# Layer 1's attention is begun inside the last query projection, its short logits share a bank, and one head's scaling changes engines

## The chip, the cores and the metric

The kernel runs on one core of a Trainium2 chip. The metric is the device time of one execution in microseconds (us). Beside the timed runs there is one execution recorded by the hardware profiler.

## The reference

Two layers of a decoder trunk act on 512 tokens of width 1024, in float32. Layer 0 mixes tokens by stick-breaking attention and a short convolution, and ends with a SwiGLU. Layer 1, where the change lies, projects the normalized input to 16 query heads, 4 key and value heads of 64, and to a small indexer with 8 heads, whose score picks 128 keys for each query:

```
dots  = einsum(q_idx, k_idx) * 64 ** -0.5
score = einsum(w_idx * 8 ** -0.5, relu(dots)), causal
idx   = top_k(score, 128)
q, k  = rms_norm(q) * q_gain, rms_norm(k) * k_gain
logits = einsum(q, k[idx]) * 64 ** -0.5 + rel_bias[bucket(q_pos - idx)]
out   = softmax(logits) @ v[idx]
x     = x + out @ w_out
```

Four query heads share one key and value head. A SwiGLU follows.

## The kernel before

All products are made of halves: each float32 operand is cut into a high part, rounded to the type that TensorE takes at speed, and a low part, the difference, and a product is three matmuls. `proj_fm` and `proj_tm` are the dense projections, and `slot` is called after each group of three such matmuls (with 512 columns). A slot is the unit of the written order: `after(n, fn, key)` puts a piece of work behind the n-th slot from now, the pieces of one slot in order of `key`. In layer 1 the scheduler is off for TensorE, VectorE, ScalarE and GpSimd, so each of them executes in the order in which the program issues; DMAs of the SP queue are placed by the scheduler.

In `layer1_mix` the stages stand in this order. The indexer's projections come first, then its scores (`dot`, `add_score`) and the choice of the largest 128 for the query blocks 1 to 3 (`largest`, `take`, lines 934 to 940), which ends in the matrices `mask`. Meanwhile keys and values, and the first eight query heads, are projected. `squares` and `head_norm` make the query norm: squares on ScalarE (line 966), a sum on VectorE (967), a reciprocal root on ScalarE (979), four small operations on VectorE, a product on GpSimd (987). `turn_q` then transposes the queries (line 999) and `stack` cuts them into halves (lines 494 and 498), the low halves of the first eight heads on GpSimd. The second eight query heads are projected next, in 32 slots (`ev_q1`, line 1173, copies its four results out), and their norm and turns follow.

Attention runs over 16 units: `order` goes through the four groups g of four heads, and in each through the four query blocks qb. A unit n has the heads 4g to 4g+3, each with (qb+1)·128 keys. Its pieces hang on b = 4n + 32 - EARLY slots, counted from the start of the last query projection:

- `logits` (lines 1064 to 1088): two matmuls of one head into a bank "z" (lines 507 and 508), of which there are two; for qb above 0 a third that adds the mask (1084); then a reduce on VectorE (1085) that adds the head's position bias, writes the sum to the tile L and the row maximum to `mx`. The bias tile of a head is loaded by a DMA of the SP queue in the unit with qb = 0 (line 1078). There are four such tiles, so the load of head h+4 waits for the last reduce of head h.
- `exps`: VectorE negates `mx` (1093), ScalarE takes four exponentials with row sums (1095).
- `norms`: one reciprocal of the four sums on VectorE (1102), and the scaling of four heads, on GpSimd (1105) or VectorE (1110) by the table NORM_POOL.
- `turn_p`: four transposes of one key block (1118), a cast on ScalarE (1129), and LAG_LO slots later the low part on VectorE (1130).
- `prod`: six matmuls with the values (lines 105 to 107) into a bank "po"; `keep` copies the unit's output out (1150, 1151).

When the query projection is over, slots pass without projection matmuls until the output projection's first half starts, 50 slots after the first unit's.

Of the kernel before, what the change touches and what calls it, by code (L numbers as in the profile page):

```python
# [8 lines left out]
F32 = mybir.dt.float32  # L9
F32R = mybir.dt.float32r  # L10
ALU = mybir.AluOpType
# [4 lines left out]
P = 128  # L16
S = 512
# [14 lines left out]
LAG_K, T1P, B2, LAG_KLO, P1 = 2, 3, 'adbc', 2, 0  # L32
EARLY, SQ_ACT = 3, 256
DOT_PACE = 1
DBL_ACT, K_POOL = True, True
PACE = (4.8, 5.0, 5.3)
NORM_POOL, NORM_ACT = (1,), (3,)
Q_POOL = ((1,), (2, 3))
EPS = 1e-6
NEG = -1e30  # L40
FILL = -3e38
# [1 line left out]
ARENA_KB = 104.5  # L43
X_SPANS = ((0, 1), (1, 2), (2, 4), (4, 6), (6, 8))

EARLY = 2
T1P = 4
LAG_K = 3
NORM_POOL = (0, 1, 3)
NORM_ACT = ()  # L50
LAG_CH = 4
LAG_TQ = 5
# [24 lines left out]
class Net:  # L77
# [762 lines left out]
    def layer1_mix(self):  # L840
        nc, I, tc = self.nc, self.I, self.tc
# [10 lines left out]
        qs, qsf = self.R(72.5, 16, S)  # L852
# [3 lines left out]
        with ExitStack() as es:  # L856
            sp = es.enter_context(tc.tile_pool(name="l1", bufs=2))
# [3 lines left out]
                    for qb in range(TB)]  # L861
            score = [None] + [wide[qb]()[:, 0] for qb in (1, 2)] + [self.ssq]
            mask = [None] + [sp.tile([P, (qb + 1) * P], F32R, name=f"mask{qb}", bufs=1)
                             for qb in (1, 2, 3)]
            eye = self.eye
# [77 lines left out]
            for qb, pace in zip((1, 2, 3), PACE):  # L943
                for r in range(16):
                    t = dots[qb] - self.slots + int(pace * r)
# [73 lines left out]
            t = head_norm(hk, [t[:, :, 1] for t in d], [t[:, :, 0] for t in d], 4, 1)  # L1019
# [40 lines left out]
            t = head_norm(h0, heads(q0[0]), heads(q0[0]), 8, 1.7)  # L1060
# [3 lines left out]
            order = [(qb, g) for g in range(4) for qb in range(TB)]  # L1064
            bias, us = {}, [{} for _ in order]

            def logits(n, r):
                (qb, g), u = order[n], us[n]
                nk = (qb + 1) * P
                t = slice(qb * P, nk)  # L1070
                h = 4 * g + r
                if r == 0:
                    u["mx"] = sp.tile([P, TB], F32, name="mx", bufs=3)
                    u["sm"] = sp.tile([P, TB], F32, name="sm", bufs=3)
                    u["ls"] = wide[qb]()
                if not qb:
                    bias[h] = sp.tile([P, S], F32, name="bias", tag="rb", bufs=4)
                    nc.sync.dma_start(bias[h], bass.AP(tensor=self.F.tensor,
                                                       offset=self.F.offset + h * 640,
                                                       ap=[[1, P], [1, S]]))  # L1080
                z = self.bank("z", "z")[:, 0:nk]
                self.qk(z, qs[:, h, t], kh[:, g, 0:nk], kl[:, g, 0:nk], not qb)
                if qb:
                    nc.tensor.matmul(z, eye, mask[qb], start=False, stop=True)  # L1084
                nc.vector.tensor_tensor_reduce(out=u["ls"][:, r], in0=z,  # L1085
                                               in1=bias[h][:, 0:nk][:, ::-1],
                                               scale=1.0, scalar=FILL, op0=ALU.add,
                                               op1=ALU.max, accum_out=u["mx"][:, r:r + 1])

            def exps(n, rs):  # L1090
                ls, mx, sm = us[n]["ls"], us[n]["mx"], us[n]["sm"]
                if rs[0] == 0:
                    nc.vector.tensor_scalar(mx, mx, -1.0, None, op0=ALU.mult)
                for r in rs:
                    nc.scalar.activation(ls[:, r], ls[:, r], AF.Exp, bias=mx[:, r:r + 1],
                                         accum_out=sm[:, r:r + 1])

            def norms(n, rs):
# [4 lines left out]
                for r in rs:  # L1103
                    if r in NORM_POOL:
                        nc.gpsimd.tensor_tensor(ls[:, r], ls[:, r],
# [39 lines left out]
            def keep(n):  # L1145
                qb, g = order[n]
                t = slice(qb * P, (qb + 1) * P)
                c = slice(2 * g, 2 * g + 2)
                po = us[n]["po"].rearrange("p (c q) -> p c q", c=2)
                nc.scalar.copy(ah[:, c, t], po)  # L1150
                self.after(LAG_K, lambda: nc.vector.tensor_tensor(
                    al[:, c, t], po, ahf[:, c, t], op=ALU.subtract), -2)

            for n, (qb, g) in enumerate(order):
                b = 4 * n + 32 - EARLY
                for r in range(4):
                    self.after(b + r, lambda n=n, r=r: logits(n, r), 0)
                for r in range(4):
                    self.after(b + 4 + r // EXPS, lambda n=n, r=r: exps(n, (r,)), 0.5)
                    self.after(b + LAG_N + r // 2, lambda n=n, r=r: norms(n, (r,)), 3)  # L1160
                for kb in range(qb + 1):
                    self.after(b + LAG_C + kb, lambda n=n, kb=kb: turn_p(n, kb), 1)
                    self.after(b + LAG_C + LAG_P + kb, lambda n=n, kb=kb: prod(n, kb), 2)
                self.after(b + LAG_C + LAG_P + qb + 1, lambda n=n: keep(n), -1)
            start = self.slots + 32 - EARLY

# [10 lines left out]
            t = head_norm(h1, heads(q1), heads(q1), 8, 1)  # L1177
# [62 lines left out]
```

## Time and profile before

| | us |
|---|---|
| median of 3 runs | 1211.86 (1211.82 to 1212.19) |
| profiled execution, its time | 1214.13 |
| profiled execution, its span | 1212.4 |
| TensorE busy | 1189.0 |
| VectorE busy | 652.9 |
| ScalarE busy | 480.1 |
| GpSimd busy | 143.8 |

The span goes from the first to the last instruction of the profiled execution; times in the trace count from its start. Matmuls are pipelined and the trace models their ends, so the starts are the safer numbers. The attention of layer 1 begins at 698 us. An idle time in brackets stands before the instruction, with what ended it.

### The profile page before, as it was taken

The numbers are of one execution on the slowest core, as the hardware profiler recorded it, in microseconds if no ns is written. First come the engines' busy times: TensorE is split into PE (matmuls) and PEld (weight loads), VectorE is DVE, ScalarE is ACT, GpSimd is POOL, SyncE is SP. The second block draws the span as 40 slices with busy tenths as digits, with TensorE's granted clock in tenths as the row PEclk, the third lists the DMA queues.
The fourth block names the chain that finished last, engine by engine and source line by source line (L and its number), as shares of the span: only waits on it lengthen the run. The fifth ranks groups of instructions, "written<-read, shape, count | busy, mean of one in ns | idle before, by whom it ended". The sixth has DMA issues, their size and how long they took to land.

```text
span 1212.4 us, 14654 instructions
## 1 busy us (share of the span) xinstructions
PE 1189.0 (98%) x5547; PEld 978.5 (81%) x5547; DVE 652.9 (54%) x1067; ACT 480.1 (40%) x797; POOL 143.8 (12%) x217
## 2 busy tenths in 40 slices
PE   9999999999999999999999989999999999999998
PEld 7777878888888888888788868888888888888886
DVE  5679965655545443333379977745444343342222
ACT  5556634543434332222253577534332322322120
POOL 1234300200000000011001554312000000000000
PEclk9999999999999999999999999999999999999999
DMA  5322125878887632232346432223333333332430
GB/s 191 92 70 70 53 84 190 277 248 281 284 273 262 226 92 96 96 96 78 124 150 232 157 104 70 71 78 126 91 89 90 103 87 102 89 104 88 129 97 35
DMA packets 118583, 159.86 MB, mean 132 GB/s; under 512 B 6292, under 2 KB 91840, under 8 KB 118512
## 3 DMA queue, kind: packets, MB, share of 16 engines
q1 hardware_dynamic: 117712, 157.73, 40.1%
q10 hardware_dynamic: 800, 1.18, 0.3%
q8 instruction: 44, 0.72, 0.2%
q14 instruction: 27, 0.22, 0.1%
HBM read 131.00 MB, written 27.89 MB: 131 GB/s over the span
## 4 chain that ended last, share of the span: by engine, by line
PE 89%; DVE 6%; issue 2%; POOL 2%; ACT 0%; DMA 0%; POOLq 0%; DVEq 0%; ACTq 0%
PE acc L105 22%; PE acc L107 21%; PE acc L106 21%; PE acc L234 6%; PE acc L233 6%; PE acc L232 6%; PE pt L1118 1%; PE z L507 1%; PE z L508 1%; DVE om L532 1%; DVE wl L163 1%; PE po L106 1%; PE po L107 1%; DVE be L535 1%; PE po L105 1%
## 5 line engine op out<-in xcount | busy, mean ns | idle before, releaser
L105 PE MATMUL acc<-arena,wh 128*128 128x512 f32 (+2 forms) x1176 | 466.7, 397 | 1.9 <-DVE xT L728 1.0
L107 PE MATMUL acc<-arena,wl 128*128 128x512 f32 (+2 forms) x1176 | 458.2, 390 | 0.1
L106 PE MATMUL acc<-arena,wh 128*128 128x512 f32 (+2 forms) x1176 | 458.0, 389 | 0.0
L163 DVE TENSOR_TENSOR wl<-raw,wh 128x1024 fp32r<-128x1024 f32 (+1 forms) x167 | 202.9, 1215 | 285.3 <-ACT wh L162 285.0
L162 ACT CAST wh<-raw 128x1024 fp32r<-128x1024 f32 (+1 forms) x167 | 173.0, 1036 | 360.5 <-PE acc L106 155.7
L107 PEld LDWEIGHTS acc<-arena,wl 128*128 128x128 f32 (+1 forms) x1176 | 220.4, 187 | 49.9 <-DVE wl L163 0.4
L105 PEld LDWEIGHTS acc<-arena,wh 128*128 128x128 f32 (+1 forms) x1176 | 220.8, 188 | 46.9 <-DVE xT L728 2.1
L106 PEld LDWEIGHTS acc<-arena,wh 128*128 128x128 f32 (+1 forms) x1176 | 220.8, 188 | 43.6 <-issue 0.7
L232 PE MATMUL acc<-wh,arena 128*128 128x512 f32 x272 | 108.8, 400 | 0.0
L234 PE MATMUL acc<-wh,arena 128*128 128x512 f32 x272 | 108.4, 399 | 0.0
L233 PE MATMUL acc<-wl,arena 128*128 128x512 f32 x272 | 108.2, 398 | 0.0
L286 POOL TENSOR_TENSOR ssq<-ssq,sqx 128x512 f32<-128x512 f32 x12 | 18.2, 1520 | 371.7 <-ACT sqx L285 371.7
L234 PEld LDWEIGHTS acc<-wh,arena 128*128 128x128 f32 x272 | 51.5, 189 | 12.2
L815 DVE TENSOR_TENSOR pwl<-praw,pwh 128x1024 fp32r<-128x1024 f32 (+1 forms) x25 | 30.2, 1208 | 57.0 <-ACT pwh L814 57.0
L233 PEld LDWEIGHTS acc<-wl,arena 128*128 128x128 f32 x272 | 51.5, 189 | 11.6
L232 PEld LDWEIGHTS acc<-wh,arena 128*128 128x128 f32 x272 | 51.5, 189 | 11.5
L763 DVE TENSOR_TENSOR ft<-acc,rbc 128x512 f32<-128x512 f32 x44 | 30.0, 690 | 45.7 <-PE acc L107 45.6
L814 ACT CAST pwh<-praw 128x1024 fp32r<-128x1024 f32 (+1 forms) x25 | 25.9, 1036 | 68.5 <-DMA praw<-in_od_w_in_dram 38.2
L765 ACT ACTIVATE fs<-ft 128x512 f32<-128x512 f32 x44 | 27.6, 629 | 51.3 <-DVE ft L763 51.3
L507 PE MATMUL z<-arena 128*128 128x384 f32 (+3 forms) x120 | 40.7, 342 | 6.7 <-DVE mx L1085 4.1
L1085 DVE CUSTOM_DVE_ANT_0 L<-z,bias 128x128 f32<-128x128 f32 (+3 forms) x64 | 30.7, 485 | 22.2 <-PE z L1084 19.6
L770 DVE TENSOR_TENSOR fp<-acc,fs 128x512 f32<-128x512 f32 x44 | 30.4, 690 | 22.7 <-PE acc L107 22.7
(212 smaller groups left out, 1281.0 us busy)
## 6 DMA issues: line engine op xcount, KB each, us to landing
raw<-in_ffn_w_gate_dram SPq DMA_DIRECT2D x44, 512.0 KB, 3.7
raw<-in_ffn_w_up_dram SPq DMA_DIRECT2D x44, 512.0 KB, 3.8
raw<-in_ffn_w_down_dram SPq DMA_DIRECT2D x42, 512.0 KB, 3.7
l1h<-pwh SPq DMA_DIRECT2D x24, 512.0 KB, 2.7
l1l<-pwl SPq DMA_DIRECT2D x24, 512.0 KB, 3.1
wh<-l1h SPq DMA_DIRECT2D x24, 512.0 KB, 4.0
wl<-l1l SPq DMA_DIRECT2D x24, 512.0 KB, 4.5
raw<-in_ev_w_in_dram SPq DMA_DIRECT2D x23, 512.0 KB, 3.9
```

Of the source, the lines that this page charges most:

```text
L105: mm(ps, wh, xh, start=first, stop=False)
L106: mm(ps, wh, xl, start=False, stop=False)
L107: mm(ps, wl, xh, start=False, stop=last)
L162: nc.scalar.copy(wh, raw)
L163: (lo or nc.vector).tensor_tensor(wl, raw, wh.bitcast(F32), op=ALU.subtract)
L232: mm(ps[tb], h[:, t], wh[:, k], start=c == 0, stop=False)
L233: mm(ps[tb], h[:, t], wl[:, k], start=False, stop=False)
L234: mm(ps[tb], l[:, t], wh[:, k], start=False, stop=c == kc - 1)
L507: self.nc.tensor.matmul(z, qs, kd, start=True, stop=False)
L770: nc.vector.tensor_tensor(p, ps, sil[m], op=ALU.mult)
L815: nc.vector.tensor_tensor(l, raw, h.bitcast(F32), op=ALU.subtract)
L1085: nc.vector.tensor_tensor_reduce(out=u["ls"][:, r], in0=z, in1=bias[h][:, 0:nk][:, ::-1], scale=1.0, scalar=FILL, op0=ALU.add, op1=ALU.max ...
```

## The change

EARLY goes from 2 to 11: everything that hangs on b moves 9 slots ahead, against the projections and the query turns, which stay. `logits` takes a tuple of heads: in units with 128 keys all four heads write to one bank and are issued in one slot, in units with 256 keys two and two; the matmuls of all heads of a bank are issued first, then their reduces. `turns`, which picks banks and tiles for the transposes, is set to -1 before the attention. NORM_POOL goes from (0, 1, 3) to (0, 1, 2).

```diff
-EARLY = 2
+EARLY = 11
 T1P = 4
 LAG_K = 3
-NORM_POOL = (0, 1, 3)
+NORM_POOL = (0, 1, 2)
...
-            def logits(n, r):
+            def logits(n, rs):
+
                 (qb, g), u = order[n], us[n]
                 nk = (qb + 1) * P
                 t = slice(qb * P, nk)
-                h = 4 * g + r
-                if r == 0:
+                if rs[0] == 0:
                     u["mx"] = sp.tile([P, TB], F32, name="mx", bufs=3)
                     u["sm"] = sp.tile([P, TB], F32, name="sm", bufs=3)
                     u["ls"] = wide[qb]()
-                if not qb:
-                    bias[h] = sp.tile([P, S], F32, name="bias", tag="rb", bufs=4)
-                    nc.sync.dma_start(bias[h], bass.AP(tensor=self.F.tensor,
-                                                       offset=self.F.offset + h * 640,
-                                                       ap=[[1, P], [1, S]]))
-                z = self.bank("z", "z")[:, 0:nk]
-                self.qk(z, qs[:, h, t], kh[:, g, 0:nk], kl[:, g, 0:nk], not qb)
-                if qb:
-                    nc.tensor.matmul(z, eye, mask[qb], start=False, stop=True)
-                nc.vector.tensor_tensor_reduce(out=u["ls"][:, r], in0=z,
-                                               in1=bias[h][:, 0:nk][:, ::-1],
-                                               scale=1.0, scalar=FILL, op0=ALU.add,
-                                               op1=ALU.max, accum_out=u["mx"][:, r:r + 1])
+                bank = self.bank("z", "z")
+                zs = [bank[:, i * nk:(i + 1) * nk] for i in range(len(rs))]
+                for r, z in zip(rs, zs):
+                    h = 4 * g + r
+                    if not qb:
+                        bias[h] = sp.tile([P, S], F32, name="bias", tag="rb", bufs=4)
+                        nc.sync.dma_start(bias[h], bass.AP(tensor=self.F.tensor,
+                                                           offset=self.F.offset + h * 640,
+                                                           ap=[[1, P], [1, S]]))
+                    self.qk(z, qs[:, h, t], kh[:, g, 0:nk], kl[:, g, 0:nk], not qb)
+                    if qb:
+                        nc.tensor.matmul(z, eye, mask[qb], start=False, stop=True)
+                for r, z in zip(rs, zs):
+                    nc.vector.tensor_tensor_reduce(out=u["ls"][:, r], in0=z,
+                                                   in1=bias[4 * g + r][:, 0:nk][:, ::-1],
+                                                   scale=1.0, scalar=FILL, op0=ALU.add,
+                                                   op1=ALU.max, accum_out=u["mx"][:, r:r + 1])
...
+            self.turns = -1
             for n, (qb, g) in enumerate(order):
                 b = 4 * n + 32 - EARLY
-                for r in range(4):
-                    self.after(b + r, lambda n=n, r=r: logits(n, r), 0)
+                w = (4, 2, 1, 1)[qb]
+                for r in range(0, 4, w):
+                    self.after(b + r, lambda n=n, rs=tuple(range(r, r + w)): logits(n, rs), 0)
```

How this moves instructions is shown at three places, as the built programs have them. Lines from 1085 on are numbered 4 higher in the changed program (1078 becomes 1082, 1084 becomes 1087).

VectorE where unit 3 ends and unit 4 begins; the first row is unit 3's last reduce, those with 128x128 are unit 4's. DMAHW3 to DMAHW6 are the bias loads. Before:

```order
L1085 ISA L,mx<-z,bias 128x512 [waits PE_49]
L1085 ISA mx 128x1
L1085 ISA L,mx<-z,bias 128x128 [waits DMAHW3_49,PE_49,Pool_49]
L1085 ISA mx 128x1
L1093 TENSOR_SCALAR mx<-mx 128x4 [waits DVE_49]
L1102 RECIPROCAL sm<-sm 128x4 [waits Activation_49]
L1130 TENSOR_TENSOR arena<-pt,arena 128x512 [waits Activation_49]
L498 TENSOR_TENSOR arena<-pt,arena 64x512 [waits Activation_49]
L498 TENSOR_TENSOR arena<-pt,arena 64x512
L1085 ISA L,mx<-z,bias 128x128 [waits DMAHW4_49,PE_49]
L1085 ISA mx 128x1
L1110 TENSOR_SCALAR L<-L,sm 128x384 [waits DVE_49]
```

Now:

```order
L1089 ISA L,mx<-z,bias 128x512 [waits PE_49]
L1089 ISA mx 128x1
L1089 ISA L,mx<-z,bias 128x128 [waits DMAHW3_49,PE_49,Pool_49]
L1089 ISA mx 128x1
L1089 ISA L,mx<-z,bias 128x128 [waits DMAHW4_49]
L1089 ISA mx 128x1
L1089 ISA L,mx<-z,bias 128x128 [waits DMAHW5_49]
L1089 ISA mx 128x1
L1089 ISA L,mx<-z,bias 128x128 [waits DMAHW6_49]
L1089 ISA mx 128x1
L1097 TENSOR_SCALAR mx<-mx 128x4 [waits DVE_49]
L1106 RECIPROCAL sm<-sm 128x4 [waits Activation_49]
```

Unit 4's four reduces now stand in one row, ahead of the negation (1093, now 1097), the reciprocal (1102, now 1106) and the low part of the turn (1130, now 1134), which stood behind the first of them.

ScalarE at the end of the last query projection; 1173 (now 1179) and 966 are a copy and squares of one of its four results, 979 is the reciprocal root of their norm. Before:

```order
L1173 COPY qn<-acc 128x512
L966 ACTIVATE sqx<-acc 128x512
L1173 COPY qn<-acc 128x512
L966 ACTIVATE sq<-acc 128x512
L979 ACTIVATE hn_y<-hn_a 128x32
L1095 ACT_TABLE_LOAD
L1095 ACTIVATE L,sm<-L,mx 128x128 x4
```

Now, from the third result on:

```order
L1179 COPY qn<-acc 128x512
L966 ACTIVATE sqx<-acc 128x512
L1099 ACTIVATE L,sm<-L,mx 128x256 x2
L1179 COPY qn<-acc 128x512
L966 ACTIVATE sq<-acc 128x512
L1099 ACTIVATE L,sm<-L,mx 128x256
L1133 CAST arena<-pt 128x512
L1099 ACTIVATE L,sm<-L,mx 128x384
L979 ACT_TABLE_LOAD
L979 ACTIVATE hn_y<-hn_a 128x32
L1099 ACT_TABLE_LOAD
L1099 ACTIVATE L,sm<-L,mx 128x384 x2
```

Exponentials now stand among the copies, with one table load ahead of the first of them, and the reciprocal root has a table load before and behind it.

GpSimd after the first eight heads' low halves (498 x8); 987 are the second query norm's products, 1105 (now 1109) the scalings of the units. Before:

```order
L498 TENSOR_TENSOR arena<-qt,arena 64x512 x8
L987 TENSOR_TENSOR qn<-qn,hn_y 128x512
L1105 TENSOR_TENSOR L<-L,sm 128x128 x2
L987 TENSOR_TENSOR qn<-qn,hn_y 128x512
L1105 TENSOR_TENSOR L<-L,sm 128x128
L987 TENSOR_TENSOR qn<-qn,hn_y 128x512 x2
L1105 TENSOR_TENSOR L<-L,sm 128x256 x3
L1105 TENSOR_TENSOR L<-L,sm 128x384 x3
```

Now:

```order
L498 TENSOR_TENSOR arena<-qt,arena 64x512 x8
L1109 TENSOR_TENSOR L<-L,sm 128x128 x3
L1109 TENSOR_TENSOR L<-L,sm 128x256 x3
L1109 TENSOR_TENSOR L<-L,sm 128x384 x2
L987 TENSOR_TENSOR qn<-qn,hn_y 128x512
L1109 TENSOR_TENSOR L<-L,sm 128x384
L987 TENSOR_TENSOR qn<-qn,hn_y 128x512 x3
L1109 TENSOR_TENSOR L<-L,sm 128x512 x3
```

The scalings of units 0 to 2 now stand ahead of the norm's products, but for the third of unit 2.

## Rows read from the trace of the kernel before

**Rows 1.** The page: the chain that ended last, shares of the span by engine.
```profile
PE 89%; DVE 6%; issue 2%; POOL 2%; ACT 0%; DMA 0%; POOLq 0%; DVEq 0%; ACTq 0%
```

**Rows 2.** Windows: stretch, busy us (instructions) by engine, granted clock, DMA share, GB/s.
```profile
700.00:705.00 5.00, 3.09 (x18) 2.13 (x17) 3.87 (x22) 2.99 (x6) 0.00 (x0) 1.00 0.63 211
705.00:710.00 5.00, 3.86 (x19) 3.05 (x20) 3.10 (x15) 3.78 (x17) 4.10 (x6) 1.00 0.01 2
735.00:740.00 5.00, 3.76 (x24) 3.12 (x22) 3.13 (x12) 3.61 (x11) 4.38 (x5) 1.00 0.71 194
740.00:745.00 5.00, 4.67 (x26) 4.37 (x27) 3.85 (x15) 4.22 (x11) 2.51 (x3) 0.71 0.66 228
```

**Rows 3.** TensorE's timeline, 690 to 709: start, us, instruction, [idle before <-releaser].
```profile
690.56 0.60 PE L999 MATMUL pt<-eye,qn 128*128 128x128 f32 x4
690.92 0.48 PE L232 MATMUL acc<-wh,arena 128*128 128x512 f32 x1
...
696.34 0.39 PE L232 MATMUL acc<-wh,arena 128*128 128x512 f32 x1
...
698.44 0.22 PE L507 MATMUL z<-arena 128*128 128x128 f32 x1
...
705.94 0.34 PE L507 MATMUL z<-arena 128*128 128x384 f32 x1
706.12 0.34 PE L508 MATMUL z<-arena 128*128 128x384 f32 x1
...
709.28 0.48 PE L507 MATMUL z<-arena 128*128 128x512 f32 x1
```

**Rows 4.** GpSimd's timeline: the low halves of the first eight heads.
```profile
688.90 11.02 POOL L498 TENSOR_TENSOR arena<-qt,arena 64x512 fp32r<-64x512 f32 x8 [2.53 <-ACT arena L494]
```

**Rows 5.** ScalarE's timeline: the table load ahead of the first exponential.
```profile
703.31 1.28 ACT L1095 ACT_TABLE_LOAD   x1
704.61 0.40 ACT L1095 ACTIVATE L<-L,mx 128x128 f32<-128x128 f32 x1
```

**Rows 6.** VectorE's timeline at the three group changes.
```profile
713.48 0.69 DVE L1085 CUSTOM_DVE_ANT_0 L<-z,bias 128x512 f32<-128x512 f32 x1 [0.18 <-PE z L1084]
...
714.63 0.29 DVE L1085 CUSTOM_DVE_ANT_0 L<-z,bias 128x128 f32<-128x128 f32 x1 [0.45 <-issue]
...
718.84 0.28 DVE L1085 CUSTOM_DVE_ANT_0 L<-z,bias 128x128 f32<-128x128 f32 x1
...
744.72 0.29 DVE L1085 CUSTOM_DVE_ANT_0 L<-z,bias 128x128 f32<-128x128 f32 x1 [0.46 <-DMA bias<-F]
...
762.31 0.69 DVE L1085 CUSTOM_DVE_ANT_0 L<-z,bias 128x512 f32<-128x512 f32 x1 [0.70 <-PE z L1084]
...
763.71 0.68 DVE L1130 TENSOR_TENSOR pT<-pt,pT 128x512 fp32r<-128x512 f32 x1
```

**Rows 7.** Bias loads issued from 708 to 716, then from 757 to 772.
```profile
DMA to landing us min/median/max: 4.3/4.3/4.3
...
DMA to landing us min/median/max: 3.0/3.0/3.1
```

**Rows 8.** Groups of instructions by form: busy us, mean ns | idle before <-releaser.
```profile
L1105 POOL TENSOR_TENSOR L<-L,sm 128x384 f32<-128x384 f32 x12 | 10.0, 860 | 10.4 <-DVE sm L1102 6.5 <-PE z L508 3.9
...
L987 POOL TENSOR_TENSOR qn<-qn,hn_y 128x512 f32<-128x512 f32 x8 | 8.2, 1046 | 15.1 <-DVE hn_y L983 15.1
```

**Rows 9.** TensorE's timeline: turns and products near the group changes.
```profile
717.74 0.62 PE L1118 MATMUL pt<-eye,L 128*128 128x128 f32 x4
...
740.05 0.33 PE L1118 MATMUL pt<-eye,L 128*128 128x128 f32 x1 [1.29 <-POOL L L1105]
...
743.34 0.31 PE L507 MATMUL z<-arena 128*128 128x128 f32 x1
...
750.34 0.33 PE L1118 MATMUL pt<-eye,L 128*128 128x128 f32 x1 [0.56 <-POOL L L1105]
...
764.44 0.38 PE L106 MATMUL po<-pT,arena 128*128 128x256 f32 x1
```

## The prediction

> **What bounds the kernel now.** I read four views in this order. The chain of waits first: TensorE makes up 89% of the chain that ended last [rows 1], so a change helps only where TensorE waits, and hurts only where it makes it wait. Then the windows: TensorE is busy throughout but for the stretch in which layer 1's attention begins; there the windows give it 3.09 and 3.86 of 5 us, and one window runs at a mean granted clock of 0.71 [rows 2]. Matmul ends are modelled, so I count from starts. Then TensorE's timeline, for which wait ends last; then the other engines' timelines there, since each works in program order and a wait holds up all that stands behind it.
>
> I number the 16 attention units 0 to 15 in program order; units 0 to 3 share four heads' bias tiles, 4 to 7 the next four. The step from 3 to 4, 7 to 8 and 11 to 12 I call a group change. The total of TensorE's matmuls does not change; from the first turn of unit 0 on its order is almost the old one. So I ask at marked places of that order how much later (or earlier) the new kernel is: its lag.
>
> **Term 1, the early start: 1.1 us gained.** Now, from the place of the new first logits (690.92 plus three matmuls, so 691.7) to unit 3's first logits at 709.28, 17.6 us go by [rows 3]. The work in it: 11 projection slots of three matmuls, 0.233 each (nine between 696.34 and 698.44), 7.7 us; two turns of 0.4 us (690.56 to 690.92); twelve logits, whose matmuls start 0.18 us apart at 384 columns (705.94 to 706.12) and, scaled, 0.12 at 256 and 0.06 at 128, 4.0 us. That makes 12.5, so 5.1 us are waits. The new order covers them with projection matmuls, but has its own. (a) Unit 0's four logits now follow the second query transpose by only some 2 us, and GpSimd does its eight low halves in 11.02 us from 688.90 [rows 4], 1.36 each: heads 0 and 1 are ready at 691.6, head 3 at 694.3. TensorE comes at 691.7 and stands until 694.4, less 0.4 of work: 2.3 us. (b) The exponentials of units 0 and 1 now stand on ScalarE between the four evacuations, after a table load of 1.28 us [rows 5]. Counting ScalarE on from that load's end at about 698.9, four copy-and-square pairs of 1.1, exponentials of 0.4 and 0.5, and a wait for VectorE's negation, the third square ends near 705.9; VectorE's sum over it (0.6) and the reduce behind it (0.5) free unit 2's last logit bank at 707.0, when TensorE has been there since 705.7: 1.4 us, and 0.2 of small waits. Together 3.9. Lag -1.1.
>
> **Term 2, the first group change: 4.2 us lost.** A bias tile of the next group reuses the buffer of this group, so its load can start only when unit 3's reduce of the same head is done. Now unit 4's four reduces are spread out: unit 3's last is at 713.48, unit 4's first at 714.63, after 0.45 us of idle time, its fourth at 718.84, and turn subtractions stand between [rows 6]. In the changed order all four stand in one row directly behind unit 3's last. The fourth then waits for a load that starts 0.1 us after that reduce's end and lands 3.0 to 4.3 us later: 4.3 for the group whose loads have a weight load behind them, 3.0 for the one that has none [rows 7]. The new SP order puts the weight loads behind the next group's four bias loads, so I take 3.0, the nearest row. Behind it wait unit 3's negated maxima, unit 2's reciprocals and unit 1's low part, for which TensorE's product waits. Worked out: unit 3's last reduce ends now at 714.1; with -1.1, and 0.6 for four small operations of the query norm that now precede it, 713.6. Bias landed 716.7, reduce 716.9, two small operations, subtraction of 0.68 [rows 6]: product at 717.8. Unit 2's reciprocals are done at 717.2; GpSimd then needs three scalings of 0.86, and its order puts a query norm of 1.05 ahead of the third [rows 8], so unit 2's first turn ends at 720.9. Now that turn starts at 717.74 [rows 9] and ends at 718.1; a query transpose (0.36) that is done by then now comes later. Lag 3.1.
>
> Some of this is there without the bias wait: the two further table loads (2.56 us) hold ScalarE up before unit 2's exponentials, so unit 1's cast ends near 715.7 (from 709.7, four exponentials of 0.6, the two loads, and 0.2, 0.25 and 0.5 for the root and two casts), and the lag would be 1.3. The load's row is followed by an activation 0.02 us after its end [rows 5], so a load is worth 1.28. The Trainium skill, "ScalarE: Activation LUTs", section "What ACT_TABLE_LOAD costs", adds a drain of 1.38 us to a load of 1.28; by that two loads cost 5.3 us, 2.8 more than I count, and the sum would rise by up to 1.5. The trace shows no such gap, and the measured load is used.
>
> **Term 3, units 5 to 7: 1.0 gained.** The shared banks leave no logit of units 4 and 5 waiting for the reduce two before it, and GpSimd's two query subtractions no longer stand between a unit's scalings. The wait that they made at 740.05 (1.29 us [rows 9]) belongs to the next term. I take 1.0; lag 2.1.
>
> **Term 4, the second group change: 0.5 lost.** Unit 7's last reduce then ends at 740.7; with 0.1, 3.0 and 0.2 the fourth reduce of unit 8 ends at 744.0; two small operations, unit 3's output subtraction (0.33) and the turn subtraction (0.68) follow, so unit 5's product runs from 745.2 to 745.9. In the trace of before it ends at 743.34 [rows 9], after that 1.29 wait and partly at the lower of the clock's two levels (1.2 instead of 2.4 GHz; 0.71 in the mean [rows 2]). That it loses little is so because the old kernel loses nearly as much here. The old one itself waits for a bias at this change: 0.46 us at 744.72 [rows 6]. By unit 7's turn, where the old kernel waits for GpSimd until 750.34 [rows 9], I come to 753.0: lag 2.6.
>
> **Term 5, the third group change: 3.0 lost.** Unit 11's last reduce ends at 762.93, the product behind it goes on at 764.44 [rows 6, 9], 1.5 us later. In the new order it is 0.1 + 3.0 + 0.2 for the bias, 0.2, 0.33 and 0.68, so 4.5 later. The output projection's first matmuls stand behind this product, so they cover nothing.
>
> **The swap of the scalings: nothing.** GpSimd had heads 0, 1, 3 and VectorE head 2; all four wait for one reciprocal of four sums, and GpSimd does three of the same size either way. The third transpose now waits instead of the fourth; one transpose (0.1 us) per such wait is lost, five times at most, which I leave in the range.
>
> **Sum.** -1.1 + 4.2 - 1.0 + 0.5 + 3.0 = +5.6 us, on the profiled execution's 1214.13 us (span 1212.4). The median of the runs shown is 2.3 us below that; 1211.86 + 5.6 gives 1217.5 us. With the landing of 4.3 instead of 3.0 three changes cost 3.9 more. The Trainium skill, "DMA: Bandwidth & Descriptors", section "Anatomy of one DMA — SWDGE (gpsimd) path", gives 2.0 us and the bytes at 436 GB/s for a load of the GpSimd queue, an estimate of 2.6 us for these 256 KB; by that the sum would be 4.4. No bias load of this trace landed below 3.0.
>
> **The rivals.** *Faster: the bias wait is not on the path* (0.14). Place: VectorE at the three changes. If what stands behind the four reduces is late anyhow, because ScalarE's casts and exponentials come later than the bias, the wait fills idle time. Price: term 2 falls by 1.8, terms 4 and 5 by 3.0 each, 7.8 in all: -2.2, so 1209.7, and a little less if the old spell of lower clock (some 2.9 of those 5 us at half) goes too. It decides for it when ScalarE's cast for the next product ends over 3 us after the last reduce. For: at the first change it ends at 715.7, 2 us after. Against: at the third TensorE went on 1.5 us after it.
>
> *No change* (0.16). The changes cost what the skipped waits and a lower landing time give back: with 2.0 less at the second and third change the sum is 1.6, so 1213.5.
>
> *Slower still* (0.15). Landing takes 4.3 us (+3.9), and stalls of 3 to 4 us of TensorE bring a spell at half clock; the one in the trace followed a window in which TensorE was busy 3.76 of 5 us [rows 2]. A spell costs up to 1.5 us: +9.5 to +11, so 1221 to 1223. For: the waits forecast are longer than the 1.29 before that spell. Against: the waits from 700 to 710 [rows 2] brought none.
>
> *The change doesn't do what it says*, that is, shared banks make TensorE wait for VectorE between logits of one bank: the built order shows logits of one bank in a row with no wait between them but for the query halves. I give it nothing of its own.
>
> **How the numbers follow.** Forecast (1214.3 to 1220): 0.55; faster 0.14; no change 0.16; slower still 0.15. A measurement of this kernel can tell 0.2%, 2.4 us, from no change. Slower by over that: 0.55 + 0.15 = 0.70; within: 0.16; faster: 0.14. The range leaves out about half of the fastest case and the end of the slowest: 1209 to 1222.5, of which 1214.3 to 1220 is the likeliest case's own.
>
> **What would show it.** Right: on VectorE at each group change the bias load named as the releaser, 2 to 3.5 us idle, and TensorE's product behind it waiting 3 us or more; TensorE's wait for GpSimd's query halves near 692, 1 us or more twice; three table loads in the attention instead of one. Wrong: no idle time of VectorE for the bias, or all of it while TensorE runs; then the sum falls to -2. A clock below 1.00 in more than one window would speak for the slowest case.

## The result and the profile after

The changed kernel takes 1226.79 us (median of 4 runs, 1226.64 to 1227.33). The kernel before, run beside it, takes 1212.03 us (4 runs). The ratio is 1.0118, with a 95% interval of 1.0101 to 1.0136: slower by 14.3 us. The forecast of 1217.5 had the sign and the places right, and the loss at less than half. The profiled execution took 1226.64 us (span 1224.9).

The page: TensorE's busy time has hardly grown (1193.6 us against 1189.0), the span by 12.5. In the second row, the chain that ended last, which is followed back over 39% of the span only, DMAs have a share of 1% where they had 0% [rows 1]; by lines that share is the load of the bias tiles.

```profile
PE 1193.6 (97%) x5547; PEld 982.9 (80%) x5547; DVE 652.1 (53%) x1067; ACT 481.9 (39%) x799; POOL 143.5 (12%) x217
...
PE 38%; DMA 1%; DVE 0%; POOL 0%; issue 0%
```

The windows of TensorE say where the time went; columns as in [rows 2], TensorE alone.

```profile
690.00:695.00 5.00, 3.41 (x17) 0.86 0.01 3
695.00:700.00 5.00, 5.00 (x24) 0.80 0.50 179
715.00:720.00 5.00, 1.66 (x7) 0.75 0.20 73
720.00:725.00 5.00, 3.85 (x19) 0.50 0.00 0
745.00:750.00 5.00, 1.55 (x8) 0.82 0.64 186
750.00:755.00 5.00, 5.00 (x24) 0.50 0.02 5
770.00:775.00 5.00, 2.74 (x22) 1.00 0.52 167
775.00:780.00 5.00, 4.30 (x20) 0.66 0.02 5
```

Each group change (713, 744 and 772 us) shows the same pair: a window in which TensorE is busy 1.55 to 2.74 of 5 us, and behind the wait a stretch at the lower of the clock's two levels, 1.2 instead of 2.4 GHz (0.75 and 0.50; 0.82 and 0.50; 0.66). Another such stretch follows the first logits (0.86 and 0.80, from 690). The trace of the kernel before had one, from 740 [rows 2].

VectorE's timeline at the three changes; each time the last 128x512 reduce of a group comes first, the 128x128 ones are the next group's.

```profile
713.65 0.68 DVE L1089 CUSTOM_DVE_ANT_0 L<-z,bias 128x512 f32<-128x512 f32 x1
...
717.63 0.29 DVE L1089 CUSTOM_DVE_ANT_0 L<-z,bias 128x128 f32<-128x128 f32 x1 [1.25 <-DMA bias<-F]
...
718.00 0.66 DVE L1134 TENSOR_TENSOR arena<-pt,arena 128x512 fp32r<-128x512 f32 x1
...
743.29 0.69 DVE L1089 CUSTOM_DVE_ANT_0 L<-z,bias 128x512 f32<-128x512 f32 x1
...
747.10 0.29 DVE L1089 CUSTOM_DVE_ANT_0 L<-z,bias 128x128 f32<-128x128 f32 x1 [1.91 <-DMA bias<-F]
...
747.96 0.29 DVE L1089 CUSTOM_DVE_ANT_0 L<-z,bias 128x128 f32<-128x128 f32 x1 [0.57 <-DMA bias<-F]
...
748.34 0.39 DVE L1155 TENSOR_TENSOR arena<-po,arena 128x256 fp32r<-128x256 f32 x1
...
771.04 0.69 DVE L1089 CUSTOM_DVE_ANT_0 L<-z,bias 128x512 f32<-128x512 f32 x1 [0.70 <-PE z L1087]
...
774.79 0.29 DVE L1089 CUSTOM_DVE_ANT_0 L<-z,bias 128x128 f32<-128x128 f32 x1 [0.92 <-DMA bias<-F]
```

This is the predicted picture: VectorE waits for the bias (0.67, 0.38 and 1.25 us at the first change, 1.91 and 0.57 at the second, 0.64 and 0.92 at the third; added up 2.3, 2.5 and 1.6, where the prediction asked for 2 to 3.5 at each), and behind the fourth reduce comes the subtraction of the turn (1134) or of the output (1155) for which TensorE stands. Here is TensorE, from the first logits to the third change:

```profile
691.01 0.33 PE L507 MATMUL z<-arena 128*128 128x128 f32 x1 [0.69 <-POOL arena L498]
...
692.34 0.33 PE L507 MATMUL z<-arena 128*128 128x128 f32 x1 [0.90 <-POOL arena L498]
...
707.26 0.44 PE L507 MATMUL z<-arena 128*128 128x384 f32 x1 [1.24 <-DVE mx L1089]
...
716.31 0.38 PE L105 MATMUL po<-arena 128*128 128x256 f32 x1 [1.55 <-ACT arena L1133]
718.72 0.58 PE L106 MATMUL po<-arena 128*128 128x256 f32 x1 [2.02 <-DVE arena L1134]
...
748.88 0.55 PE L105 MATMUL po<-arena 128*128 128x256 f32 x1 [3.45 <-DVE arena L1155]
...
775.70 0.55 PE L105 MATMUL po<-arena 128*128 128x256 f32 x1 [2.96 <-DVE arena L1155]
```

It waits 0.69 and 0.90 us for GpSimd's query halves, 1.24 us for a logit bank, 1.55 us for a cast of ScalarE at the first change, and then 2.02, 3.45 and 2.96 us at the three changes for a low part (of a turn or of an output) on VectorE that stands behind the fourth bias.

To see what each place costs I count, in every kernel, from the same matmul of layer 1's projections (669.3 us in the kernel before) to the last product matmul of a unit; the dense matmuls ahead of it are the same in all kernels. The table gives how much later than in the kernel before that is (worked out from start times of one trace of each):

| lag in us at the end of unit | 0 | 4 | 7 | 11 | 15 |
|---|---|---|---|---|---|
| after | +0.9 | +5.9 | +10.7 | +14.4 | +14.5 |
| `merge_only` | -0.2 | +5.8 | +10.1 | +14.0 | +14.0 |
| `early_only` | -2.9 | -0.8 | -1.7 | -1.6 | -1.6 |
| `merge_unit0` | +0.9 | +3.8 | +3.2 | +2.9 | +3.0 |
| `spread` | 0.0 | +2.5 | +2.5 | +2.7 | +2.8 |
| `filler` | -0.3 | +3.3 | +6.8 | +9.8 | +9.9 |

So the start cost 0.9, the first change 5.0, the second with what lies before it 4.8, the third 3.7. Behind that nothing is added. The spans differ by 12.5 only, since the trace of the kernel before reaches the matmul from which I count 1.9 us later than that of the changed kernel.

### The profile page after: what moved, and what is told of

Same layout as the page of the kernel before. It is cut to its first block, busy times and chain, and to the rows that moved or that the text cites. A ratio compares the mean times of both kernels' runs of the same rounds, so it can differ in the third digit from the quotient of the medians.

```text
span 1224.9 us, 14641 instructions
## 1 busy us (share of the span) xinstructions
PE 1193.6 (97%) x5547; PEld 982.9 (80%) x5547; DVE 652.1 (53%) x1067; ACT 481.9 (39%) x799; POOL 143.5 (12%) x217
## 5 line engine op out<-in xcount | busy, mean ns | idle before, releaser
L1099 ACT ACTIVATE L<-L,mx 128x128 f32<-128x128 f32 (+3 forms) x64 | 35.8, 561 | 29.8 <-DVE sm L1106 25.4
```

## The experiments

All were timed in five rounds beside the kernel before; ratios are to it. What a ratio lies above or below 1, times 1212 us, is the difference in us that I give. The edits shown are against the changed kernel, or against the kernel that the text names; `...` marks what is left out.

**Three parts of the change, each alone.**

`merge_only`: the new `logits` alone.

```diff
-EARLY = 11
+EARLY = 2
...
-NORM_POOL = (0, 1, 2)
+NORM_POOL = (0, 1, 3)
...
-            self.turns = -1
```

> The kernel before with the new logits function alone (four heads of a 128-key unit and two of a 256-key unit share a bank); EARLY 2, the old scaling table and the old turn counter. Theory (the merged reduces of a group's first unit wait for the bias loads, and each such wait of TensorE is followed by a spell at the lower clock): VectorE waits 2 us or more for the bias load at each of the three group changes, TensorE stands 3 to 4 us at each and runs some microseconds at a clock below 1.00 behind it; 1219 to 1224 us. Rival (the early start makes most of the loss: the wait for GpSimd's query halves with its spell, and the table loads): 1211 to 1216 us, no half-clock spell at the group changes.

Measured: 1228.23 us, ratio 1.0128 (1.0114 to 1.0142), +15.5 us. The bias waits are all there (three at the first change, at most 1.00 us; 2.38 at the second; 0.95 at the third), and so is the low clock:

```profile
720.00:725.00 5.00, 4.85 (x22) 0.50 0.00 0
745.00:750.00 5.00, 1.25 (x12) 0.67 0.59 193
```

The whole loss comes with the shared banks, and it is 4 us above the top of what I expected. The rival, that the early start makes most of it, falls.

`early_only`: the early start alone (and the turn counter's new start, which was not tried by itself).

```diff
-NORM_POOL = (0, 1, 2)
+NORM_POOL = (0, 1, 3)
...
-                w = (4, 2, 1, 1)[qb]
+                w = (1, 1, 1, 1)[qb]
```

> The kernel after with the heads of every unit on their own (one head per bank and slot) and the old scaling table, so that of the change the 9 slots and the turn counter are left. Theory: the bias loads are as well covered as before (one wait of about 0.5 us on VectorE per group change), what is left is the wait for GpSimd's query halves near 691 us with its spell at the lower clock of some 3 us, against 5 us of waits covered: 1210 to 1214 us. Rival (the early start makes most of the loss): 1219 us or more.

Measured: 1211.05 us, ratio 0.9990 (0.9982 to 0.9999), -1.2 us. It has one bias wait of 0.47 us and no wait for GpSimd's halves at all: one head per slot comes late enough for them. So the early start as such is a small gain. The time is within the span that I gave, but the wait for the halves that I had expected is not there.

`swap_only`: NORM_POOL alone, on the kernel before.

```diff
-NORM_POOL = (0, 1, 3)
+NORM_POOL = (0, 1, 2)
```

> The kernel before with the new scaling table alone (GpSimd takes heads 0, 1, 2 and VectorE head 3). Theory: within 1.5 us of the kernel before (1210.5 to 1213.5 us). Rival (GpSimd's third scaling now ends later than VectorE's did and the transposes wait for it, as the trace after shows one wait of 1.15 us for it): 1215 us or more.

Measured: 1212.76 us, ratio 1.0001 (0.9992 to 1.0010). The swap is worth nothing, as forecast.

**Which shared bank costs.**

`unmerge128`: only the units with 256 keys share.

```diff
-                w = (4, 2, 1, 1)[qb]
+                w = (1, 2, 1, 1)[qb]
```

> The kernel after with only the 128-key units back to one head per bank and slot; the 256-key units keep two heads in a bank, EARLY 11 and the new table stay. Theory: the bias wait goes back to about 0.5 us per change, the three half-clock spells behind it go with it, 1210 to 1215 us, with the spell near 694 us left. Rival (the 256-key merge or the early start costs as much as the 128-key merge): 1219 us or more.

Measured: 1213.25 us, ratio 1.0008 (0.9999 to 1.0017). Against `early_only` the pairs (with the swap) cost 0.0018, 2.2 us. The four-head units make the rest, 0.0110 or 13.3 us. The low clock that I expected near 694 is not in this trace (1.00 from 685 to 710); one at the first change is (0.50 from 715 to 720).

`merge_unit0`: of the four-head units unit 0 alone, which waits for no bias.

```diff
-                w = (4, 2, 1, 1)[qb]
+                w = (1 if n else 4, 2, 1, 1)[qb]
```

> The kernel after with four heads in a bank in unit 0 alone, where no bias load is waited for; the other 128-key units have a bank per head, the 256-key units two heads. It is the kernel unmerge128 (1213.25 us) but for unit 0. Theory (with four heads at once TensorE waits for GpSimd's query halves near 691 us, about 2 us, and a spell at the lower clock may follow): 1214 to 1216 us. Rival (the merge costs only where a bias load stands before it): within 0.7 us of unmerge128.

Measured: 1215.33 us, ratio 1.0022 (1.0013 to 1.0031), 1.7 us above `unmerge128`. TensorE's timeline and windows show what unit 0 pays for: both waits for the query halves, and a low clock behind them. (This profiled execution took 1217.75 us, 2.4 above the median, so the median may hold less of the low clock.)

```profile
693.53 0.33 PE L507 MATMUL z<-arena 128*128 128x128 f32 x1 [0.68 <-POOL arena L498]
...
694.88 0.42 PE L507 MATMUL z<-arena 128*128 128x128 f32 x1 [0.91 <-POOL arena L498]
...
718.90 0.58 PE L105 MATMUL po<-arena 128*128 128x256 f32 x1 [1.25 <-ACT arena L1133]
```

```profile
695.00:700.00 5.00, 5.00 (x18) 0.66 0.01 3
...
720.00:725.00 5.00, 4.60 (x22) 0.50 0.00 0
```

What is left for units 4, 8 and 12 is 1.0118 - 1.0022, 11.6 us: nearly four per group change in the mean. By the table they are not even: what the changed kernel loses beyond `merge_unit0` is 2.1 us at the first change, 5.4 at the second and 4.0 at the third. At the first, `merge_unit0` itself loses 2.9, behind 1.25 us of waiting for ScalarE's cast and at the low clock (both above), so more than half of the 5.0 there is not due to the four-head unit.

**The row of reduces, and the bias in it.**

`spread`: logits share banks as in the change, but the reduces go back to one per slot, in all units, and the line that loads a head's bias goes with its reduce.

```diff
-                for r, z in zip(rs, zs):
-                    nc.vector.tensor_tensor_reduce(out=u["ls"][:, r], in0=z,
...
+                for r in range(4):
+                    self.after(b + r, lambda n=n, r=r: reduce(n, r), 0.1)
```

> The kernel after with one thing undone: the matmuls of the heads that share a bank are still issued together in one slot, but the reduces go back to one per slot (head r at b + r), as before. The full bias tiles and four buffers stay. Theory (what costs is the row of four reduces on VectorE, which makes everything behind it wait for the fourth bias load; the shared bank itself is harmless): the idle time of VectorE for the bias load falls to about 0.5 us per change, 1210 to 1215 us. Rival (the shared banks cost, because logits no longer stand between the other matmuls and cover the casts): 1217 us or more, with the bias wait small and TensorE waiting for casts (arena, pt) instead.

Measured: 1216.01 us, ratio 1.0028 (1.0018 to 1.0038): 10.9 us better than after, and within the intervals of `merge_unit0`. It lies 1 us above the span that I gave to the theory. VectorE at the first change:

```profile
713.84 0.29 DVE L1093 CUSTOM_DVE_ANT_0 L<-z,bias 128x128 f32<-128x128 f32 x1
...
716.30 0.28 DVE L1093 CUSTOM_DVE_ANT_0 L<-z,bias 128x128 f32<-128x128 f32 x1
...
718.16 0.28 DVE L1093 CUSTOM_DVE_ANT_0 L<-z,bias 128x128 f32<-128x128 f32 x1
```

The first reduce of unit 4 still comes 0.8 us behind unit 3's last; the other three now come 2.5 to 4.5 us behind the first, when their loads have landed, and not one wait for a bias is left in this stage. The loads themselves are not earlier: the last one at the first change is issued 4.4 us behind the first and lands 3.2 us later, as in the changed kernel. So at a group change the shared bank is harmless; the four reduces in one row, each waiting for its load, are what costs.

`short_bias`: the row stays, the wait for the bias goes. Units 4, 8 and 12 read 128 columns of bias from `ssq`, which is idle there, loaded two units ahead.

```diff
+            short = lambda r: self.ssq[:, r * P:(r + 1) * P]
...
+                if qb == 2 and rs[0] == 0 and g < 3:
+                    for r in range(4):
+                        nc.sync.dma_start(short(r), bass.AP(
+                            tensor=self.F.tensor,
+                            offset=self.F.offset + (4 * g + 4 + r) * 640,
+                            ap=[[1, P], [1, P]]))
...
+                    add = bias[4 * g + r][:, 0:nk] if qb or not g else short(r)
...
-                                                   in1=bias[4 * g + r][:, 0:nk][:, ::-1],
+                                                   in1=add[:, ::-1],
```

> The kernel after, merging and all, but the 128-key units of groups 1 to 3 read their bias from four 128-column tiles in ssq (idle at that time) that are loaded some eight slots earlier; the full tiles are still loaded at the group change, for the 256-key unit that follows. Theory (the wait for the bias loads is what the merge adds): the releaser DMA bias<-F before the reduces of a 128-key unit is gone, the half-clock spells of 10.2, 6.8 and 3.4 us at the group changes go or shrink, 1208 to 1213 us. Rival (the merged units stand for another reason too: four heads in one bank delay the bank's release, or GpSimd's scalings): 1217 us or more.

Measured: 1217.45 us, ratio 1.0040 (1.0027 to 1.0053), 9.4 us better than after, but 4.5 above the top of the theory's span and just inside the rival's. Both are partly right. At the second change (in a profiled execution of 1220.60 us, 3.2 above the median) the four reduces now follow one another with no bias wait:

```profile
744.47 0.29 DVE L1097 CUSTOM_DVE_ANT_0 L<-z,ssq 128x128 f32<-128x128 f32 x1 [0.69 <-issue]
744.69 0.08 DVE L1097 DVE_READ_ACCUMULATOR2_ANT mx<- 128x1 f32 x1
...
745.11 0.08 DVE L1097 DVE_READ_ACCUMULATOR2_ANT mx<- 128x1 f32 x1
...
745.48 0.40 DVE L1163 TENSOR_TENSOR arena<-po,arena 128x256 fp32r<-128x256 f32 x1
```

Against `merge_unit0`, which has no four-head unit at a change, 0.0018 or 2.2 us are left. I put them down to the row itself, since VectorE is busy with four reduces while TensorE waits 0.79 us for the output subtraction behind them (1163 in this kernel). So of the 11.6 us some 9.4 are the bias loads and 2.2 the row; the two intervals just overlap, and the second number could be near nothing.

`short_bias_unmerged`: the same with a bank for every head.

```diff
-                w = (4, 2, 1, 1)[qb]
+                w = (1, 1, 1, 1)[qb]
```

> The kernel with the short bias tiles, and every head in a bank and slot of its own. It tells what the merge is worth when no bias load stands before it. Theory: the merge alone neither gains nor loses over 2 us once the bias is there, so this is within 2 us of the merged kernel with short bias tiles, and of the kernel with only the early start (1211 us). Rival (the merge frees TensorE of bank waits and is worth 3 us or more): this kernel is 3 us or more above the merged one.

Measured: 1211.06 us, ratio 0.9984 (0.9975 to 0.9993). It equals `early_only` within the intervals, as expected: where the reduces are spread the bias was hardly waited for. But the merged kernel with short tiles is 6.8 us slower, so the first half of what I expected was wrong: merging loses even with the bias there, by the row (2.2), unit 0 (1.7) and the pairs (2.2), which are 6.1 of these 6.8.

**The clock.**

`filler`: after, and 13 matmuls that nobody reads behind unit 4's, 8's and 12's logits.

```diff
+            def fill():
+                z = self.bank("z", "z")
+                for i in range(13):
+                    nc.tensor.matmul(z, eye, mask[3], start=True, stop=True)
...
+                if not qb and g:
+                    self.after(b + 1, fill, 0)
```

> The kernel after, with 13 matmuls of 128x512 whose result nobody reads (some 3.0 us of TensorE at full clock) behind the four logits of the 128-key unit at each of the three group changes, where TensorE waits. The bias loads and VectorE's wait stay as they are. Theory that splits the loss (waits of 3 to 4 us each, and on top of that the lower clock behind them): the waits are filled, the clock stays at 1.00 at the three changes, and with 39 matmuls more the kernel is faster than after, 1217 to 1221 us. Rival (the time goes with the waits alone, the clock costs nothing): 1226 us or more.

Measured: 1223.40 us, ratio 1.0089 (1.0075 to 1.0104). 39 matmuls more, and 3.5 us faster than after (the two intervals just overlap). TensorE at the first change, and the windows behind the first two:

```profile
714.21 3.24 PE L1161 MATMUL z<-mask,eye 128*128 128x512 f32 x13
...
718.31 0.39 PE L106 MATMUL po<-arena 128*128 128x256 f32 x1 [0.74 <-DVE arena L1134]
```

```profile
715.00:720.00 5.00, 3.87 (x19) 1.00 0.21 58
750.00:755.00 5.00, 4.39 (x39) 1.00 0.28 90
```

The fillers take the place of the wait, and the clock stays at 1.00. The products that wait do not start sooner for it: from the end of unit 4 to unit 5's first product (747.27 here, 748.88 in after) the lag grows by 3.4 us in both; what is gained lies behind these starts. So I put the 3.5 us down to the low clock (what the fillers themselves delay isn't told apart). The table of lags has it by place: from unit 0 to 4, 4 to 7 and 7 to 11 `filler` loses 3.6, 3.5 and 3.1 us, after 5.0, 4.8 and 3.7, so the clock makes 1.4, 1.3 and 0.7. The larger part, some 8 of the 11.6 us, is the waits themselves; it may be somewhat more, since `merge_unit0` too has the low clock at the first change. I had expected 1217 to 1221, and so given the clock too much.

`early_fill`: the same idea in `early_only`, which waits 1.25 and 1.23 us at its first change.

```diff
+            def fill(k):
+                z = self.bank("a", "z")
+                for i in range(k):
+                    nc.tensor.matmul(z, eye, mask[3], start=True, stop=True)
...
+                if n == 4:
+                    self.after(b + 2, lambda: fill(6), 1)
+                    self.after(b + 3, lambda: fill(5), 0.5)
```

> The kernel with only the early start (1211.05 us), which had one spell of 6.8 us at the lower clock behind two waits of TensorE of 1.25 us at the first group change, with 6 and 5 unread matmuls of 128x512 put into these two waits (2.6 us of TensorE at full clock). Theory (the clock falls behind waits and costs on its own): the spell is gone, 1208.5 to 1210.5 us, faster for more work. Rival (the waits are not what brings the spell, or the fill takes as long as the spell costs): 1211 us or more.

Measured: 1210.47 us, ratio 0.9984 (0.9974 to 0.9993), against 0.9990 for `early_only`: not told apart. The window behind the first wait in `early_only`, then in this kernel:

```profile
715.00:720.00 5.00, 4.00 (x19) 0.53 0.00 0
```

```profile
715.00:720.00 5.00, 4.38 (x34) 1.00 0.00 0
```

The low clock (0.53) is gone, and the trace is only 0.5 us ahead at the end of unit 4. Here, where TensorE waits for others anyway, the low clock was nearly free.

**Other start times.** `short_bias_e9` sets EARLY to 9 in `short_bias`.

```diff
-EARLY = 11
+EARLY = 9
```

> The merged kernel with short bias tiles, EARLY 9 in place of 11, so that the first unit's logits come after GpSimd's first query halves. Theory: the two waits for the halves near 691 us (about 2 us) are gone, two slots of cover at the end of the projection are lost (up to 2.3 us): within 1.5 us of the same kernel with EARLY 11. Rival (the wait near 691 us brings a spell of the lower clock that costs 1.5 us more): faster by 2 us or more.

Measured: 1223.58 us, ratio 1.0083 (1.0070 to 1.0096): 5.2 us slower where I expected no more than 1.5. The waits for the halves are gone, but with less projection behind them the logits of unit 2 wait for their bank three times, 0.71, 0.73 and 2.08 us, and a stretch at the lower clock follows (0.66 from 705 to 715). By the traces this is 2.2 us at the end of unit 0; another 2.8 come between the ends of units 4 and 7, where TensorE waits 2.16 us for an output subtraction at 747.38, and why is not shown.

`early14` sets EARLY to 14 in `early_only`.

```diff
-EARLY = 11
+EARLY = 14
```

> The kernel with only the early start (unmerged, old scaling table; 1211.05 us), its first unit 14 slots ahead in place of 11. Theory (what the early start is worth is the waits that projection matmuls cover; at 11 slots some 1 to 2 us of small bank waits are left between 698 and 711 us, and the first logits would now come while GpSimd still cuts the first query halves): the two cancel, 1210 to 1213 us. Rival (the query halves are 3 slots, 2 us, further from ready, and the wait comes in full with a spell of the lower clock): 1213.5 us or more. Third possibility (the softmax of the first units is off ScalarE before the two table loads of the query norm): 1209 us or less.

Measured: 1218.97 us, ratio 1.0054 (1.0040 to 1.0068): the rival's number, but not by its mechanism alone. The wait for the halves came back (1.33 and 1.09 us), without the low clock (1.00 up to 750), but at the end of unit 4 the trace is still 0.5 us ahead of the kernel before; at the end of unit 7 it is 5.6 behind. Most is lost at 748 us, where the second query half's low parts on GpSimd now fall between the scalings of one unit. GpSimd, then TensorE:

```profile
745.69 2.22 POOL L1109 TENSOR_TENSOR L<-L,sm 128x512 f32<-128x512 f32 x2 [4.00 <-PE z L1087]
747.99 2.61 POOL L498 TENSOR_TENSOR arena<-qt,arena 64x512 fp32r<-64x512 f32 x2
750.67 1.04 POOL L1109 TENSOR_TENSOR L<-L,sm 128x512 f32<-128x512 f32 x1
```

```profile
751.77 0.48 PE L1122 MATMUL pt<-eye,L 128*128 128x128 f32 x1 [3.36 <-POOL L L1109]
```

Two slots less (in the merged kernel) and three more thus cost several times what the whole early start brings.

## Why the prediction was wrong

The mechanism was right in its main part: the row of reduces makes VectorE wait for the bias loads, TensorE's products stand behind, and the sizes of single waits were close. What failed is the price of the second group change, and that the low clock behind each stall stood at nothing in the sum. The sum came out at +5.6 and is +14.5 in the trace. By terms:

- **Term 1 (-1.1; measured +0.9).** The waits came as worked out: 0.69 and 0.90 us for the halves (2.0 between starts, 2.3 forecast) and 1.24 for the logit bank (1.4). What I left out of the sum is the low clock behind the first (0.86, 0.80). In the traces without it, `filler` and `spread`, the lag at unit 0 is -0.3 and 0.0, so it cost about 1 us; another 0.8 to 1.1 between these lags and -1.1 is not explained (0.1 of it is rounding: 3.9 from 5.1 is 1.2). That `early_only` ends 1.2 us ahead does not confirm the 1.1, and the likeness is chance: it has no wait for the halves, is 2.9 ahead at the end of unit 0 (the term without its 2.3 for the halves is -3.4), and then loses part of that at the first change.
- **Term 2 (+4.2; measured +5.0).** Unit 3's last reduce ends at 714.33, the fourth bias is used at 717.63, 3.3 us later; I had 3.1. The product's second matmul starts at 718.72, and from it on the product runs at the low clock. Without that clock the term was 3.6 (`filler`), so the waits were even a little shorter than forecast. The part of the term that I gave to ScalarE and GpSimd without the bias (-1.1 to 1.3, so 2.4) is 2.9 in `merge_unit0`.
- **Terms 3 and 4 (-1.0 and +0.5; measured +4.8).** This is the step that failed. The chain after unit 7's last reduce was sized well: 743.98 to the product at 748.88 are 4.9 us, I had 4.5. But the same stretch in the kernel before, whose bias wait of 0.46 comes only behind it (744.72), is much shorter:

```profile
739.08 0.08 DVE L1085 DVE_READ_ACCUMULATOR2_ANT mx<- 128x1 f32 x1
...
741.61 0.35 PE L105 MATMUL po<-arena 128*128 128x256 f32 x1
...
743.13 0.41 PE L107 MATMUL po<-arena 128*128 128x256 f32 x1
```

From 739.16 to 741.61 are 2.45 us, so the wait adds 2.45, not 0.5. I compared the *ends* of the two products, 745.9 and 743.34 [rows 9]. The old product took 1.5 us from its first matmul to its last, mostly at the lower clock, and I let the new one take 0.7 at full clock; but behind a longer stall it runs at the lower clock too (748.88 to 750.41, 1.5 us again). By starts my own numbers, 745.2 and 741.61, lie 3.6 apart, where I carried 2.6 on. (The 740.7 that I started from was also only 1.5 behind the old 739.16, though the lag carried to it was 2.1.) And term 3's gain did not come: between unit 4's products and unit 7's last reduce the lag grew by 0.9, from 5.9 to 6.8, since two query subtractions of VectorE now stand ahead of unit 7's last two reduces:

```profile
741.25 1.39 DVE L498 TENSOR_TENSOR arena<-pt,arena 64x512 fp32r<-64x512 f32 x2 [0.36 <-ACT arena L494]
```

`merge_unit0` has them too, and its lag grows from 3.8 to 4.7 there. The low clock through 750 to 755 (0.50) makes some 1.3 of the 4.8, as `filler` has it.
- **Term 5 (+3.0; measured +3.7).** The bias comes 3.1 us after the reduce as forecast; the clock in the window behind it (0.66) adds the rest, 0.7 by `filler`.
- **The swap: nothing**, and measured so (1.0001).

There are three table loads in the attention now, as forecast. For the two further ones the trace bears out the price used: a load of 1.28 us, the next activation 0.01 to 0.02 us behind it.

```profile
712.32 1.28 ACT L1099 ACT_TABLE_LOAD   x1
713.62 0.62 ACT L1099 ACTIVATE L<-L,mx 128x384 f32<-128x384 f32 x1
```

The Trainium skill, "ScalarE: Activation LUTs", section "What ACT_TABLE_LOAD costs", adds a drain of 1.38 us; these rows show none. By it my sum would have been nearer to the result, for a reason that is not there.

The landing was 3.0 to 3.9 us: at the second and third change

```profile
DMA to landing us min/median/max: 3.7/3.8/3.9
...
DMA to landing us min/median/max: 3.0/3.2/3.4
```

so the 3.0 that I took was the lower end, and the 4.3 of [rows 7] was not reached. The estimate of 2.6 us from the Trainium skill, "DMA: Bandwidth & Descriptors", section "Anatomy of one DMA — SWDGE (gpsimd) path", is below every one of them; it is stated for loads of the GpSimd queue, and these are loads of the SP queue.

Of the rivals, *slower still* named the missing mechanism, the lower clock behind each stall, with a chance of 0.15 and a price of 1.5 us for a spell; I had asked for a low clock in more than one window as its sign, and eight windows of 5 us show it. It is right in kind, but `filler` puts the clock at 3.5 us of the changes' 11.6, and the 4.3 us landing did not come, so its 1221 to 1223 is short as well. *Faster* falls: at each change TensorE's product waits for an operation of VectorE that stands behind the last bias wait. *No change* falls with it.

What stays open: whether the low clock follows a given wait is not the same from one of these traces to the next. `swap_only`, which differs from the kernel before by one table entry, has it from 700 to 710 (0.75 and 0.91) and not from 740. `merge_unit0` and `spread` have the same two waits between 691 and 695 us (0.7 and 0.9 us), yet only the first has the low clock behind them (0.66, above); in `spread` the same window reads:

```profile
695.00:700.00 5.00, 5.00 (x29) 1.00 0.60 213
```

A share of about 1 us of the comparisons by trace hangs on this; the ratios above rest on medians.

## What to carry to other kernels

When several reads of buffers that are about to be reloaded are issued in one row, the last one waits for the whole latency of its load (here it came 3.1 to 4.0 us behind the read that set its buffer free), and everything behind it on that engine waits too. Spread the reads, as the kernel before did, or give the first short use a small buffer of its own. And when a stall is priced, start from the same event in the old and the new trace, and compare starts: the end of a piece of work that ran at half clock is no measure of the wait ahead of it.

No variant beats the kernel before by over 0.2%: `early_only`, `short_bias_unmerged` and `early_fill` stand at 0.9984 to 0.9990. They are the ones to keep from this change: the early start without the shared banks.

## What was not expected of the hardware

Adding 39 matmuls of 128x512 made the changed kernel 3.5 us faster, since the clock then stayed at 1.00 through the attention. The price of a low clock was not the same in two of these kernels: 3.5 us where TensorE's products led the path, under 1 us (0.9990 to 0.9984, not told apart) in `early_only`, where TensorE waited for ScalarE and GpSimd at the same time. That this is the reason for the difference was argued, not tested.
